# A two-layer hybrid decoder on one core: the second mixer's steps handed out in smaller portions, half of a set of weight sums moved to GpSimd in a later stage, and the value product's weight splits reordered

## The chip, the cores and the metric

The kernel runs on one core of one Trainium2 chip. The metric is device time in microseconds (us) of one execution; lower is better. The engines are named as in the profile: PE is TensorE, PEld its weight loads, DVE is VectorE, ACT is ScalarE, POOL is GpSimd, SP is SyncE, whose queue issues nearly all DMAs here.

## The reference, cut to what matters

The input is 1024 positions of 1024 channels in fp32. Two residual layers follow each other, each a token mixer and a SwiGLU feed-forward, and a last RMSNorm.

```python
for layer in range(2):
    hn = rms_norm(h, norm_mix_g[layer])
    h = h + (mixer_ab if layer == 0 else mixer_cd)(hn, ...)
    hn = rms_norm(h, norm_ffn_g[layer])
    h = h + (silu(hn @ w_gate) * (hn @ w_up)) @ w_down
...
def mixer_cd(h, w_in, lower_bound, norm_g, w_out):
    hq, hf, hi, hg, sq, sk, sv = split_cols(h @ w_in, CD_SPLITS)
    o_c = hgrn2_recurrence(silu(hq), k_in, hi, log_f)       # 4 heads
    o_c = rms_norm(o_c, norm_g) * sigmoid(hg)
    # three dilated windows of attention over sq, sk, sv, 4 heads each, joined by a softmax of their sums
    return concatenate([o_c, o_d]) @ w_out
```

## The kernel before

**Products.** Weights and activations are fp32. Each is split into a rounded part and a rest (`split`, lines 103 and 104: one ACT cast, one DVE subtraction), and each product is three matmuls of 128x128 weights on 512 columns (`mm3`, lines 136 to 138: hi with hi, hi with lo, lo with hi; the third of each group is the first to read the weights' rest).

**Seven products for eight.** The gate and up projections (`Up`), and most of the second mixer's input projection (`Local`), are computed by a scheme of the Strassen kind: two weight blocks and two halves of positions are combined by sums so that seven products of a quarter each do for eight. Both run as a loop of "pairs". One pair is 84 matmuls. Inside it the order of PE, DVE, ACT, POOL and SP is written out by hand (`manual_schedule`): every engine, and SP's queue of DMAs, takes its instructions in the order in which the function `pair` names them. `Local` has pairs 3 to 15 in its loop (15 is the last); the products of one pair run in the order `p1`, `p2`, `end21` and `end12` of the pair before, `p6`, `p5`, `p7`. `p6` and `p5` need the weights `s2`, `s1`, which come from `sums(an, bn)` (POOL, lines 338 and 339, issued late in the pair before), then `part_b` (an ACT cast and a DVE subtraction). `sums` needs the raw weight block `bn`, whose load SP issues in the middle of a pair (`raw`, line 311). `sums_late` (POOL, lines 343 and 344) makes two more. In pairs 12 to 15 four results go through `rope`: two ACT copies, a POOL multiplication (line 873), then a DVE addition that is only issued at the next `flush`.

**The value weights' sums.** The product that makes the recurrence's values (`rows`) uses the same scheme on four weight blocks. Their sums `vsum`, two halves of 1024 columns, are made earlier, in layer 0's `Up`: `block_load` brings 256 columns of four blocks into the single buffer `sd`, `block_sums` runs four DVE operations and stores the result. The same two functions also make `Up`'s own 22 blocks of `w_down` sums. In the pairs of `more` (4 to 15 in layer 0) they run a second time in the pair.

**rows.** After the last pair, `rows` runs the value product, `v_ask` loading a raw weight, `v_unit` splitting it into one of four ring buffers. It ends with the splits of `t1`, needed later by the mixer.

**The second mixer** (`mixer_cd`). Two generators are interleaved with plain projections: `hgrn` (the recurrence, 80 steps) and `local` (attention). `tick(cost)` gives each a credit (3.5 and 2 or 2.5 per 24 matmuls, capped at 3) and runs as many steps as the credit pays. `swa_v` and `hgrn_gates` call it between groups of matmuls. Here no order is written by hand: the tile scheduler orders the instructions by its own estimate, those named earlier first.

Of the kernel before, what the change touches and what calls it, by code (L numbers as in the profile page):

```python
# [56 lines left out]
def hybrid_trunk_kernel(ctx: ExitStack, tc: tile.TileContext, x_t, w_all, w_down, w_ba, vecs, c_f, c_i, c_rope, out):  # L57
# [233 lines left out]
    class Up:  # L291
# [168 lines left out]
        def block_load(self):  # L460
            n = self.blocks - ND // SB
            if n < (0 if self.layer else 2 * DM // SB):
                a = self.right.tile([P, 4, SB], F32, tag="sd", name="sd", bufs=1)
                if n < 0:
                    c = slice(self.blocks * SB, (self.blocks + 1) * SB)
                    dma(a, w_down[self.layer].rearrange("x y p n -> p (x y) n")[:, :, c])
                    d = self.sums_d.rearrange("s p n -> p s n")[:, :, c]
                else:
                    i, c = n // (DM // SB), slice(n % (DM // SB) * SB, (n % (DM // SB) + 1) * SB)
                    for j, at in enumerate(VSETS):  # L470
                        dma(a[:, j], w_all[W_AT["cd", at + i]][:, c])
                    d = vsum[:, i].rearrange("s p n -> p s n")[:, :, c]
                self.block = d, a
                self.blocks += 1
# [30 lines left out]
        def pair(self, f, b11, b21, b22, t1, t2, t3, t4):  # L505

            n = f + 1
            more = (5, 7, 9, 11) if self.layer else range(4, 16)
            self.p1(f, b11)
# [254 lines left out]
    class Local(Up):  # L764

        def __init__(self, left):
            self.left, self.n = left, 0
            self.qk = {k: dr.tile([2 if k[0] is not None else 4, P, T_LEN], F32, name=f"qk{i}")
                       for i, k in enumerate(PAIRS)}
            self.b12 = dr.tile([P, KH, HT], F32, name="b12")  # L770
            self.units = {f: {} for f in range(len(PAIRS) + 1)}
            self.x, self.y, self.z, self.u2, self.g1, self.c22 = {}, {}, {}, {}, {}, {}
            self.snaps = self.right = None
            self.adds, self.stores, self.decays = [], [], {}

        def source(self, kind, f):
# [173 lines left out]
        def run(self, tr, row, b11, b21, hx, close, left, right):  # L950

            self.early(hx)
            E = mybir.EngineType
            engines = {E.PE, E.DVE, E.Activation, E.Pool}
            with tc.manual_schedule(engines=engines):
                b22, t3, t4 = self.turn(tr, row, b11, b21, hx, close, left, right)
            t1, t2 = self.t12
            with tc.manual_schedule(engines=engines | {E.SP}):
                last = len(PAIRS) - 1
                for f in range(3, last + 1):  # L960
                    self.pair(f, f == last, b11, b21, b22, t1, t2, t3, t4)
                self.copy22(last)
                self.add22(last)
                self.end21(last, t4)
                self.rope22(last)
                self.v_unit()
                self.end12(last, b22)
                self.rows(last, b11, b21, b22, t1, t2, t3, t4)
            return [t1, b22], self.vu[14:]

        def v_ask(self):
            i = len(self.vraw)
            if i < 14:
                name, k = ("cd", 8), i % 2
                blk = (8, 10, 0, 2, 3, 1, 46)[i // 2]
                src = w_all[W_AT["cd", blk + k]] if blk >= 8 else vsum[blk, k]
            elif i < 16:
                src = w_all[W_AT["cd", 48 + i - 14]]
            raw = self.left.tile([P, DM], F32, tag="spare", name="raw", bufs=1) if i % 3 == 0 else \
                ring.tile([P, DM], F32, tag="raw", name="raw", bufs=2)  # L980
            dma(raw, src)
            self.vraw.append(raw)

# [6 lines left out]
        def rows(self, last, b11, b21, b22, t1, t2, t3, t4):  # L990
# [9 lines left out]
            def zt():  # L1000
                return self.right.tile([P, HT], F32, tag="z", name="z", bufs=3)

            x = [psu(), psu()]
            for j in range(2):
                prod(x[j], 0, b11, j, first=True)
            self.rope21(last)
            self.add12(last)
            self.v_ask()
            self.v_unit()
            self.rope12(last)  # L1010
            self.v_ask()
            x += [psu(), psg()]
            for j in range(2, 4):
                prod(x[j], 0, b11, j, first=True)
            self.v_unit()
            while self.adds or self.stores:
                self.flush()
            self.v_ask()

            g, y = [], []  # L1020
            for j in range(4):
                y.append(psm())
                prod(y[j], 2, b21, j, first=True, end=True)
                g.append(zt())
                S.copy(g[j], x[j])
                if j > 1:
                    self.v_unit()
                    self.v_ask()
                V.tensor_tensor(g[j], g[j], y[j], op=ADD)
                store(3, 0, j, g[j])  # L1030

            u2 = []
            for n in range(2):
                for j in range(4):
                    prod(x[j], 4, t2, j, range(2 * n, 2 * n + 2))
                if n == 0:
                    self.v_unit()
                    self.v_ask()
            for j in range(4):
                u2.append(self.scratch("u2"))  # L1040
                S.copy(u2[j], x[j])
            self.v_unit()
            self.v_ask()
            for n in range(2):
                for j in range(4):
                    prod(x[j], 6, t3, j, range(2 * n, 2 * n + 2))
                self.v_unit()
                self.v_ask()

            def late(j):  # L1050
                c = self.right.tile([P, HT], F32, tag="c", name="c", bufs=2)
                S.copy(c, x[j])
                return c

            for a in (0, 2):
                z = []
                for j in (a, a + 1):
                    z.append(psm())
                    prod(z[-1], 8, t1, j, first=True)
                    c = late(j)  # L1060
                    V.tensor_tensor(c, c, z[-1], op=ADD)
                    store(1, 1, j, c)
                if a == 0:
                    self.v_unit()
                    self.v_unit()
                    self.v_ask()
                    self.v_ask()
                else:
                    self.v_unit()
                    self.v_unit()  # L1070
                    back = [ring.tile([P, DM], F32, tag="raw", name="raw", bufs=2) for _ in range(2)]
                    for i, raw in enumerate(back):
                        dma(raw.rearrange("p (k t) -> p k t", k=2), self.b12[:, 2 * i:2 * i + 2, :])
                for i, j in enumerate((a, a + 1)):
# [3 lines left out]
            for j in range(4):  # L1078
                prod(x[j], 12, t4, j, end=True)
                if j < 2:  # L1080
                    c = slice(2 * j, 2 * j + 2)
                    split(t1[0][:, c, :], t1[1][:, c, :], back[j].rearrange("p (k t) -> p k t", k=2))
                if j == 1:
                    self.v_ask()
                    self.v_ask()
                c = zt()
                S.copy(c, x[j])
                store(1, 0, j, c)
                if j > 1:
                    self.v_unit()  # L1090

        def pair(self, f, last, b11, b21, b22, t1, t2, t3, t4):
# [8 lines left out]
            else:  # L1101
                self.vraw, self.vu = [], []
                self.v_ask()
                self.v_ask()
            self.add22(f - 1)
            self.decay(f - 1, 4)
            self.part_b(f, self.s)
            self.sums_late(self.a, self.b, self.s)
            self.p2(f, b21, psm())
            g = self.snap(f)  # L1110
# [9 lines left out]
            self.p6(f, t2)  # L1120
            self.rope21(f - 1)
            self.part_d(f, self.a)
            self.decay(f - 1, 6)
            if not last:
                bn = self.raw("u", n, n % 3 == 2)
            self.add12(f - 1)
            if not last:
# [4 lines left out]
            if last:  # L1132
                self.v_unit()
                self.v_ask()
            self.rope12(f - 1)
# [954 lines left out]
    def mixer_cd(hn, hp, qkd, wv):  # L2090
# [5 lines left out]
        with ExitStack() as es:  # L2096
# [16 lines left out]
            def halves_of(w, half, tick):  # L2113
                o = proj(w, hn[half], range(KH), last=False)
                tick(0.5)
                return proj(w, hn[half], range(KH, KT), o, first=False)

# [147 lines left out]
            def hgrn_gates(tick):  # L2265
                ws = [wload(("cd", 12 + 2 * i), ("cd", 13 + 2 * i)) for i in range(2)]
                for h in range(4):
                    for half in range(NH):
# [7 lines left out]
                        gate_store[0] = dma(catd[half][h], xg).ins  # L2276
                        tick(0.5)


            def swa_v(p, tick, w=()):  # L2280
# [14 lines left out]
                for tts in ((0, 1, 2), (3,), (4,), (5, 6, 7)):  # L2295
                    os_ = [psu() for _ in tts]
                    for ks in ((range(0, 2), range(2, 4), range(4, 6), range(6, 8)) if len(tts) > 1 else (range(KT),)):
                        for tt, o in zip(tts, os_):
                            part(o, tt, ks)
                        tick(0.75 if len(tts) > 1 else 1)  # L2300
                    for tt, o in zip(tts, os_):
# [540 lines left out]
```

## Time and profile before

| | us |
|---|---|
| three runs | 2521.59, 2521.28, 2519.64 |
| median of the runs | 2521.28 |
| the profiled execution | 2526.62 |
| its span, first to last instruction | 2524.5 |

The span is what the rows below are taken from; the profiled execution has 2.1 us more around it and is 5.3 us above the median of the runs. PE is busy for 2491.4 us of the span.

### The profile page before, as it was taken

How to read it: one execution, taken by the hardware profiler on the slowest of the kernel's cores; microseconds unless marked ns; L12 is line 12 of the kernel's file. 1: busy time of each engine (PE TensorE's matmuls, PEld its weight loads, DVE VectorE, ACT ScalarE, POOL GpSimd, SP SyncE). 2: the span in 40 equal slices, each digit the busy share in tenths (PEclk: the TensorE clock that was granted, in tenths of full speed). 3: DMA queues.
4: the chain of work that ended last, by engine and by line, in shares of the span. 5: the costliest groups of instructions: out<-in, count | busy, mean ns of one | idle time of the engine just before them, and what ended most of it. 6: DMA issues, size and time to landing. Idle time of an engine off the chain costs nothing. (4 is left out here: it accounts for less than half of the span.)

```text
span 2524.5 us, 37197 instructions
## 1 busy us (share of the span) xinstructions
PE 2491.4 (99%) x13715; PEld 2062.4 (82%) x13715; DVE 1695.4 (67%) x2823; ACT 1100.7 (44%) x1932; POOL 637.4 (25%) x591
## 2 busy tenths in 40 slices
PE   9999999999999999999999999999999999999998
PEld 7888888888887888888888877788788888888887
DVE  8987776676566565567798636678668565656554
ACT  5432134343333344344676535567535333334442
POOL 1311112333333400031566300010132333330001
PEclk9999999999999999999999999999999999999999
DMA  4535457335667688544344456776732555668853
GB/s 156 163 121 169 133 174 264 104 117 193 207 226 238 215 302 292 183 139 137 129 142 153 138 174 219 185 211 195 255 134 93 183 184 192 204 213 287 277 177 125
DMA packets 296526, 467.20 MB, mean 185 GB/s; under 512 B 50168, under 2 KB 151064, under 8 KB 296088
## 3 DMA queue, kind: packets, MB, share of 16 engines
q1 hardware_dynamic: 296056, 464.31, 56.6%
q8 instruction: 107, 1.75, 0.3%
q10 hardware_dynamic: 288, 0.52, 0.1%
q14 instruction: 75, 0.61, 0.1%
HBM read 314.18 MB, written 150.55 MB: 184 GB/s over the span
## 5 line engine op out<-in xcount | busy, mean ns | idle before, releaser
L104 DVE TENSOR_TENSOR w<-raw,w 128x1024 fp32r<-128x1024 f32 (+1 forms) x333 | 400.4, 1205 | 155.0 <-ACT w L103 153.5
L103 ACT CAST w<-raw 128x1024 fp32r<-128x1024 f32 (+1 forms) x333 | 315.3, 954 | 280.6 <-PE psu L138 126.2
L136 PE MATMUL psu<-hnh,w 128*128 128x512 f32 x772 | 308.3, 399 | 0.0
L138 PE MATMUL psu<-hnh,w 128*128 128x512 f32 x772 | 301.3, 390 | 0.0
L137 PE MATMUL psu<-hnl,w 128*128 128x512 f32 x772 | 301.3, 390 | 0.0
L199 POOL TENSOR_TENSOR acc<-acc,sq 128x512 f32<-128x512 f32 x52 | 78.8, 1516 | 440.3 <-ACT sq L195 440.2
L338 POOL TENSOR_TENSOR ws<-raw 128x512 f32<-128x512 f32 x54 | 71.2, 1319 | 452.3 <-DMA raw<-in_dram 271.5
L136 PEld LDWEIGHTS psu<-hnh,w 128*128 128x128 f32 x772 | 145.1, 188 | 31.0 <-ACT sq L195 0.8
L138 PEld LDWEIGHTS psu<-hnh,w 128*128 128x128 f32 x772 | 145.0, 188 | 30.9
L137 PEld LDWEIGHTS psu<-hnl,w 128*128 128x128 f32 x772 | 145.2, 188 | 28.2
L104 DVE TENSOR_TENSOR hidq<-hr,hidq 128x1024 fp32r<-128x1024 f32 x72 | 82.3, 1145 | 78.7 <-ACT hidq L103 78.4
L104 DVE TENSOR_TENSOR w<-ws,w 128x1024 fp32r<-128x1024 f32 x51 | 71.8, 1408 | 89.8 <-ACT w L103 89.8
L103 ACT CAST hidq<-hr 128x1024 fp32r<-128x1024 f32 x72 | 70.2, 980 | 103.2 <-DMA hr<-ts 62.4
L429 POOL TENSOR_TENSOR hid<-hid,c 128x512 f32<-128x512 f32 x44 | 64.7, 1470 | 168.6 <-ACT hid L428 168.5
L136 PE MATMUL psm<-hidq,w 128*128 128x512 f32 (+1 forms) x275 | 106.1, 386 | 0.0
L137 PE MATMUL psm<-hidq,w 128*128 128x512 f32 (+1 forms) x275 | 105.8, 385 | 0.0
L138 PE MATMUL psm<-hidq,w 128*128 128x512 f32 (+1 forms) x275 | 105.8, 385 | 0.0
L136 PE MATMUL psu<-t3h,w 128*128 128x512 f32 x240 | 93.8, 391 | 4.4 <-ACT u L401 4.3
L381 ACT ACTIVATE gt<-gt 128x512 f32<-128x512 f32 x44 | 27.8, 632 | 155.2 <-DVE gt L378 155.2
L136 PE MATMUL psu<-t4h,w 128*128 128x512 f32 x240 | 93.5, 390 | 0.8 <-ACT c L890 0.8
L137 PE MATMUL psu<-t3l,w 128*128 128x512 f32 x240 | 93.4, 389 | 0.0
L137 PE MATMUL psu<-t4l,w 128*128 128x512 f32 x240 | 93.4, 389 | 0.0
(614 smaller groups left out, 6700.6 us busy)
## 6 DMA issues: line engine op xcount, KB each, us to landing
raw<-in_dram SPq DMA_DIRECT2D x223, 512.0 KB, 4.4
sd<-in_dram SPq DMA_DIRECT2D x44, 512.0 KB, 4.0
hid<-hid SPq DMA_DIRECT2D x88, 256.0 KB, 3.3
sd<-sd SPq DMA_DIRECT2D x44, 512.0 KB, 3.0
hr<-ts SPq DMA_DIRECT2D x40, 512.0 KB, 4.7
raw<-sd SPq DMA_DIRECT2D x40, 512.0 KB, 4.7
qk<-z SPq DMA_DIRECT2D x52, 256.0 KB, 3.1
hd<-h SPq DMA_DIRECT2D x48, 256.0 KB, 2.9
```

The costliest lines, as they stand in the source:

```text
L103: S.copy(hi, src)
L104: eng.tensor_tensor(lo, src, hi.bitcast(F32), op=SUB)
L136: T.matmul(o, lh, rh, start=first and i == 0, stop=False, **kw)
L137: T.matmul(o, lh, rl, start=False, stop=False, **kw)
L138: T.matmul(o, ll, rh, start=False, stop=last and i == n - 1, **kw)
L199: (eng or G).tensor_tensor(a, a, q, op=ADD)
L338: G.tensor_tensor(s[:, HT:], b[:, :HT], b[:, HT:], op=ADD)
L381: S.activation(self.g1[f], self.g1[f], AF.Silu)
L429: G.tensor_tensor(h, h, self.c22.pop(f), op=MULT)
```

## The change

Three edits. (1) `tick` is called behind every six matmuls with a quarter of the cost, in `swa_v` and in `hgrn_gates`; the sum of the costs is the same. (2) Layer 0's `Up` makes only the first half of `vsum`; its second calls in a pair end at pair 11. The other half is loaded in `Local`, in pairs 13 and 14, as eight blocks of 128 columns, four DMAs each, and is summed by POOL: each `v_sums` runs four POOL operations and a store per block loaded since the last one. (3) The loads and splits of the value product are asked for earlier and more evenly, its raw weights have four buffers and not three, and the product's first half moves ahead of the last pair's `end21` and `end12`.

```diff
         def block_load(self):
             n = self.blocks - ND // SB
-            if n < (0 if self.layer else 2 * DM // SB):
+            if n < (0 if self.layer else DM // SB):
...
-            more = (5, 7, 9, 11) if self.layer else range(4, 16)
+            more = (5, 7, 9, 11) if self.layer else range(4, 12)
...
+        def v_load(self, f):
+            for i in range(2 if 13 <= f < 15 else 0):
+                n = len(self.vblocks)
+                c = slice(n * P, n * P + P)
+                a = self.scratch("vs").rearrange("p (s n) -> p s n", s=4)
+                for j, at in enumerate(VSETS):
+                    dma(a[:, j], w_all[W_AT["cd", at + 1]][:, c])
+                self.vblocks.append((a, vsum[:, 1].rearrange("s p n -> p s n")[:, :, c]))
+
+        def v_sums(self):
+            t = G.tensor_tensor
+            for a, d in self.vblocks[self.vdone:]:
+                t(a[:, 3], a[:, 2], a[:, 3], op=ADD)
+                t(a[:, 2], a[:, 0], a[:, 2], op=SUB)
+                t(a[:, 0], a[:, 3], a[:, 0], op=SUB)
+                t(a[:, 1], a[:, 1], a[:, 0], op=SUB)
+                dma(d, a)
+            self.vdone = len(self.vblocks)
...
+        def v_raw(self):
+            i = len(self.vraw) % 4
+            raw = ring.tile([P, DM], F32, tag="raw", name="raw", bufs=2) if i in (1, 2) else \
+                self.left.tile([P, DM], F32, tag=("spare", None, None, "s")[i], name="raw", bufs=1)
...
+            def nxt():
+                self.v_unit()
+                self.v_ask()
...
             x = [psu(), psu()]
+            self.copy22(last)
+            self.add22(last)
             for j in range(2):
                 prod(x[j], 0, b11, j, first=True)
+            self.end21(last, t4)
+            self.rope22(last)
+            self.end12(last, b22)
             self.rope21(last)
             self.add12(last)
-            self.v_ask()
-            self.v_unit()
+            nxt()
...
             self.part_b(f, self.s)
             self.sums_late(self.a, self.b, self.s)
+            self.v_sums()
+            self.v_load(f)
             self.p2(f, b21, psm())
...
             self.rope21(f - 1)
+            self.v_sums()
+            self.v_load(f)
             self.part_d(f, self.a)
             self.decay(f - 1, 6)
             if not last:
                 bn = self.raw("u", n, n % 3 == 2)
+            else:
+                self.v_ask()
+                self.v_ask()
...
             if last:
-                self.v_unit()
-                self.v_ask()
+                for _ in range(2):
+                    self.v_unit()
+                    self.v_ask()
...
             def halves_of(w, half, tick):
-                o = proj(w, hn[half], range(KH), last=False)
-                tick(0.5)
-                return proj(w, hn[half], range(KH, KT), o, first=False)
+                o = psu()
+                for k in range(0, KT, 2):
+                    if k:
+                        tick(0.25)
+                    proj(w, hn[half], range(k, k + 2), o, first=k == 0, last=k == KT - 2)
+                return o
...
-                        tick(0.5)
+                        tick(0.25)
...
-                    for ks in ((range(0, 2), range(2, 4), range(4, 6), range(6, 8)) if len(tts) > 1 else (range(KT),)):
+                    for ks in (range(0, 2), range(2, 4), range(4, 6), range(6, 8)):
                         for tt, o in zip(tts, os_):
                             part(o, tt, ks)
-                        tick(0.75 if len(tts) > 1 else 1)
+                            tick(0.25)
```

## Rows read from the trace of the kernel before

**Rows 1.** The page, span and busy times of PE

```profile
span 2524.5 us, 37197 instructions
...
PE 2491.4 (99%) x13715; PEld 2062.4 (82%) x13715; DVE 1695.4 (67%) x2823; ACT 1100.7 (44%) x1932; POOL 637.4 (25%) x591
```

**Rows 2.** Stretches: us, busy by engine (xcount), granted clock, DMA share, GB/s

```profile
740.00:830.00 90.00, 85.61 (x374) 69.61 (x373) 57.95 (x79) 30.98 (x44) 34.97 (x24) 1.00 0.70 229
...
1190.00:1364.00 174.00, 174.00 (x770) 144.06 (x769) 145.04 (x167) 127.19 (x180) 99.65 (x66) 1.00 0.44 142
...
1422.00:1515.00 93.00, 89.63 (x483) 73.02 (x482) 39.85 (x53) 34.04 (x46) 6.96 (x8) 1.00 0.52 174
1515.00:1800.00 285.00, 269.47 (x3142) 227.43 (x3141) 214.09 (x753) 179.00 (x517) 26.19 (x47) 0.98 0.70 202
1542.70:1549.50 6.80, 6.03 (x17) 4.98 (x18) 1.94 (x6) 3.49 (x11) 0.00 (x0) 0.50 0.63 192
1631.40:1638.30 6.90, 5.12 (x92) 4.38 (x93) 6.48 (x18) 5.30 (x15) 1.69 (x4) 0.51 0.50 162
```

**Rows 3.** In order of time, layer 0's `Up`: start, duration, instruction, [idle before, releaser]

```profile
770.59 1.76 SPq L471 DMA_DIRECT2D sd<-in_dram  x4
...
776.37 0.43 DVE L479 TENSOR_TENSOR sd<-sd 128x256 f32<-128x256 f32 x1 [5.29 <-DMA raw<-in_dram]
...
785.63 0.50 PE L136 MATMUL psu<-t3h,w 128*128 128x512 f32 x1 [1.95 <-ACT u L401]
```

**Rows 4.** PE's waits from 1360 to 1515: us in total, times, longest

```profile
PE psm L137 <- DVE w L104: 1.8, 1, 1.8
PE psu L136 <- ACT c L890: 0.8, 1, 0.8
```

**Rows 5.** In order of time, `Local`, pairs 13 and 14

```profile
1380.50 1.29 POOL L873 TENSOR_TENSOR sw<-sw,rope 128x512 f32<-128x512 f32 x1 [2.76 <-ACT sw L872]
...
1382.41 0.33 SPq L311 DMA_DIRECT2D raw<-in_dram  x1
...
1386.65 1.29 POOL L338 TENSOR_TENSOR ws<-raw 128x512 f32<-128x512 f32 x1 [1.05 <-DMA raw<-in_dram]
...
1390.43 1.22 DVE L104 TENSOR_TENSOR w<-ws,w 128x1024 fp32r<-128x1024 f32 x1 [4.55 <-ACT w L103]
1390.53 2.28 POOL L344 TENSOR_TENSOR raw<-raw,ws 128x512 f32<-128x512 f32 x1
...
1394.76 0.39 PE L136 MATMUL psu<-t2h,w 128*128 128x512 f32 x1
```

**Rows 6.** Groups on POOL by shape: busy us, mean ns of one, idle before

```profile
L338 POOL TENSOR_TENSOR ws<-raw 128x512 f32<-128x512 f32 x54 | 71.2, 1319 | 452.3 <-DMA raw<-in_dram 271.5 <-DVE hid L456 77.5 <-DVE gt L378 45.2
...
L1917 POOL COPY yt<-yd 32x128 f32<-32x128 f32 x32 | 10.6, 343 | 35.0 <-DMA yd<-scr_y 26.8 <-DVE y L1867 7.5
...
L2005 POOL TENSOR_TENSOR ss<-ss,s_nq 128x4 f32<-128x4 f32 x8 | 2.1, 267 | 57.3 <-ACT oq L1999 57.3
```

**Rows 7.** SP's queue, its waits from 1360 to 1425

```profile
SPq L311 <- DVE w L104: 10.3, 2, 5.3
```

**Rows 8.** PE's waits in the second mixer, 1510 to 1800

```profile
PE psg L2259 <- DVE e L2254: 2.2, 3, 1.2
PE psg L2225 <- ACT e L2220: 1.9, 2, 1.1
```

**Rows 9.** PE in order of time: two waits, and a visit to small matmuls

```profile
1513.61 0.50 PE L138 MATMUL psu<-w,hnl 128*128 128x512 f32 x1
1513.95 0.39 PE L136 MATMUL psu<-w,hnh 128*128 128x512 f32 x1
1514.27 0.76 PE L2158 MATMUL psg<-m 128*32 128x32 f32 x64
...
1543.47 0.69 PE L2418 MATMUL psm<-cf,sc 128*128 128x128 f32 x2 [2.71 <-ACT sc L2375]
...
1631.69 0.66 PE L2158 MATMUL psg<-m 128*32 128x32 f32 x32 [2.86 <-DVE m L2150]
```

More of the change, by code (lines that the diff above doesn't have):

```diff
@@ L468, in block_load @@
                 else:
-                    i, c = n // (DM // SB), slice(n % (DM // SB) * SB, (n % (DM // SB) + 1) * SB)
+                    c = slice(n * SB, (n + 1) * SB)
                     for j, at in enumerate(VSETS):
-                        dma(a[:, j], w_all[W_AT["cd", at + i]][:, c])
-                    d = vsum[:, i].rearrange("s p n -> p s n")[:, :, c]
+                        dma(a[:, j], w_all[W_AT["cd", at]][:, c])
+                    d = vsum[:, 0].rearrange("s p n -> p s n")[:, :, c]
                 self.block = d, a
@@ L774, in __init__ @@
             self.adds, self.stores, self.decays = [], [], {}
+            self.vblocks, self.vdone = [], 0
         def source(self, kind, f):
@@ L961, in run @@
                     self.pair(f, f == last, b11, b21, b22, t1, t2, t3, t4)
[L962 to L965, printed above, removed]
-                self.v_unit()
-                self.end12(last, b22)
                 self.rows(last, b11, b21, b22, t1, t2, t3, t4)
             return [t1, b22], self.vu[14:]
-        def v_ask(self):
[L972 to L982, printed above, removed]
+        def v_load(self, f):
[19 more added lines that the diff above has]
+                self.left.tile([P, DM], F32, tag=("spare", None, None, "s")[i], name="raw", bufs=1)
+            self.vraw.append(raw)
+            return raw
+        def v_ask(self):
+            i, k = len(self.vraw), len(self.vraw) % 2
+            blk = (8, 10, 0, 2, 3, 1, 46, 48)[i // 2]
+            dma(self.v_raw(), w_all[W_AT["cd", blk + k]] if blk >= 8 else vsum[blk, k])
         def v_unit(self):
@@ L1001, in zt, with back @@
                 return self.right.tile([P, HT], F32, tag="z", name="z", bufs=3)
+            def nxt():
+                self.v_unit()
+                self.v_ask()
+            def back(n):
+                dma(self.v_raw().rearrange("p (k t) -> p k t", k=2), self.b12[:, 2 * n:2 * n + 2, :])
             x = [psu(), psu()]
+            self.copy22(last)
+            self.add22(last)
             for j in range(2):
                 prod(x[j], 0, b11, j, first=True)
+            self.end21(last, t4)
+            self.rope22(last)
+            self.end12(last, b22)
             self.rope21(last)
             self.add12(last)
-            self.v_ask()
-            self.v_unit()
+            nxt()
             self.rope12(last)
-            self.v_ask()
             x += [psu(), psg()]
@@ L1014, in rows @@
                 prod(x[j], 0, b11, j, first=True)
-            self.v_unit()
+            nxt()
             while self.adds or self.stores:
                 self.flush()
-            self.v_ask()
             g, y = [], []
@@ L1025, in rows @@
                 S.copy(g[j], x[j])
-                if j > 1:
-                    self.v_unit()
-                    self.v_ask()
                 V.tensor_tensor(g[j], g[j], y[j], op=ADD)
                 store(3, 0, j, g[j])
+                if j > 1:
+                    nxt()
             u2 = []
@@ L1036, in rows @@
                 if n == 0:
-                    self.v_unit()
-                    self.v_ask()
+                    nxt()
             for j in range(4):
@@ L1041, in rows @@
                 S.copy(u2[j], x[j])
-            self.v_unit()
-            self.v_ask()
+            nxt()
             for n in range(2):
@@ L1046, in rows @@
                     prod(x[j], 6, t3, j, range(2 * n, 2 * n + 2))
[L1047 to L1053, printed above, removed]
+                nxt()
+                if n == 1:
+                    nxt()
             for a in (0, 2):
@@ L1059, in rows @@
                     prod(z[-1], 8, t1, j, first=True)
-                    c = late(j)
+                    c = self.right.tile([P, HT], F32, tag="c", name="c", bufs=2)
+                    S.copy(c, x[j])
+                    if j == 0:
+                        nxt()
                     V.tensor_tensor(c, c, z[-1], op=ADD)
                     store(1, 1, j, c)
-                if a == 0:
+                if a:
+                    nxt()
                     self.v_unit()
[L1065 to L1073, printed above, removed]
+                    back(0)
                 for i, j in enumerate((a, a + 1)):
@@ L1080, in rows @@
                 if j < 2:
[L1081 to L1085, printed above, removed]
+                    self.v_unit()
+                    if j == 0:
+                        back(1)
                 c = zt()
@@ L1088, in rows @@
                 store(1, 0, j, c)
-                if j > 1:
-                    self.v_unit()
+            for n in range(2):
+                c = slice(2 * n, 2 * n + 2)
+                split(t1[0][:, c, :], t1[1][:, c, :], self.vraw[16 + n].rearrange("p (k t) -> p k t", k=2))
         def pair(self, f, last, b11, b21, b22, t1, t2, t3, t4):
@@ L1103, in pair @@
                 self.v_ask()
-                self.v_ask()
             self.add22(f - 1)
@@ L1132, in pair @@
             if last:
-                self.v_unit()
-                self.v_ask()
+                for _ in range(2):
+                    self.v_unit()
+                    self.v_ask()
             self.rope12(f - 1)
```

## The prediction, made before the changed kernel ran

> **What bounds the kernel.** The page first: PE is busy for 2491.4 us of a span of 2524.5 [rows 1]. The change takes no matmul away, so all it can win is PE's idle time, 33.1 us, and time at a lower clock; all it can lose is new waits. The stretches come next [rows 2]. In `Local` from 1190 to 1364 PE is never idle: 770 matmuls in 174 us, 0.226 us each, so a pair of 84 takes 19.0 us. Idle time lies in three places that the change touches: layer 0's `Up` from 740 to 830 (90.0 less 85.6: 4.4 us), `rows` from 1422 to 1515 (3.4 us) and the second mixer from 1515 to 1800 (15.5 us). In the mixer the granted clock also stood at 0.5, which is 1.2 GHz, for two spells of 6.8 and 6.9 us; PE's busy part of them, 6.0 and 5.1 us, would take half as long at 2.4 GHz: 5.6 us more. The reader is to see that everything to be won is about 29 us, and that `Local` has nothing to win.
>
> **Layer 0's Up.** The idle time there begins at the buffer `sd`: SP spends 1.76 us on issuing the four loads of one block of `vsum`, DVE stands for 5.29 us until the loads of that time have landed (the profile names a raw load), and PE's `p7` then waits 1.95 us for an ACT copy that is queued behind DVE's late work [rows 3]. The edit takes four such blocks away and gives each pair from 12 on one block where it had two, so that a load has half a pair or more before DVE asks. I take the whole 4.4 us as won: **-4.4** (bounds 0, if another load is late in its place, and -4.4). DVE's 16 operations and 16 loads that go are hidden under PE and win nothing themselves.
>
> **rows.** Two waits go [rows 4]. The 0.8 us for ACT's copy of the last pair's sum goes because 24 matmuls are put between it and `end21`. The 1.8 us for a split is that of the two weights of `b22`, which were both split after the first products of `t1`; in the new order the later of them is split 12 matmuls ahead. **-2.6** (bounds 0 and -2.6). Behind it the splits of `t1` come last, but their first use is after two sets of projections in the mixer, over 20 us later.
>
> **The second mixer.** The sum of the credits is the same, but bursts go: two attention steps in a row, or `ms1` and `od1` of the recurrence in a row, now have 12 matmuls between them, and every other two steps of one generator at least six. The two longest waits are of just this kind: 2.71 us for exponentials just issued and 2.86 us for `m` [rows 9]; two more groups, 2.2 and 1.9 us, wait for a result of the step just before [rows 8]. They won't all go: DVE is busy for 214 of 285 us [rows 2], and the tile scheduler had already moved matmuls between steps where it foresaw a wait (the visit at 1514.27 lies in the middle of a group). I take two thirds of 15.5 us: **-10** (bounds: nothing, and all 15.5). Each spell at half clock began beside one of the two long waits; without them I count the clock as full: **-5.6** (bounds 0 and -5.6). Against it stand more changes between big and small matmuls. Counted through the code, 36 groups of matmuls were followed by a step with work for PE, and now some 70 are. Around a visit one big matmul takes 0.34 and one 0.32 us to the next start [rows 9] where 0.226 is normal: 0.21 us together, of which most visits, to wider small matmuls, should pay about half. 34 times 0.1: **+3.4** (bounds 0 and 7).
>
> **Local, the sums on POOL.** No row shows a 128x128 sum on POOL. A two-operand POOL instruction takes 0.27 us with 4 columns and 1.29 to 1.32 us with 512 [rows 5, 6]; on the line between them 128 columns take 0.51. Eight, for the two blocks of one `v_sums`, take 4.1 us. Bounds: 0.34 each, as a copy of 128 columns [rows 6], and 0.64, a quarter more, since `sums_late` beside busy DVE took 2.28 instead of 1.29 [rows 5]. I take 0.51, the line through the same kind of instruction. The GPSIMD Engine Reference of the Trainium skill (section 3.1) speaks against such sums on this engine and gives 4497 ns for 2048 columns; scaled down with no fixed cost that is an estimate of 0.28 us each, and by it the `Local` term below would be about 9 us instead of 16.8; the trace's 1.29 us for 512 columns, where that scale gives 1.12, speaks for a fixed cost on top.
>
> These 32 operations are on POOL, which has room for one `v_sums` a pair, but what counts is SP. SP's queue takes its DMAs in order and already stands for 10.3 us in two waits of raw loads [rows 7]. In pairs 13 and 14 the second `v_sums` puts two stores, which wait for POOL, and eight loads in front of the load of `bn`, and `bn` is what the next pair's `sums` needs.
> - Pair 13: POOL's third rope multiplication ends at 1381.8; eight sums, 4.1, to 1385.9; one store 0.4 and eight loads at 0.44 [rows 3], 3.5, to 1389.8. There `bn` is issued, before at 1382.4. From issue to POOL's first sum took 4.2 us (1382.41 to 1386.65), and from there to the end of the split 5.0 (1391.65) [rows 5]: 1399.0. `p6` begins at 1394.76 and its third matmul needs the split's rest 0.45 later: a wait of 3.8 us. Behind the waiting ACT cast stand the copy of `p1` and the ropes, so nothing else feeds PE meanwhile.
> - Pair 14 has four blocks, and POOL and SP form a loop: `sums` and `sums_late` 6.2 (1386.65 to 1392.81), four-operation sums of two blocks 4.1, two ropes 2.6, ACT's copies 0.6, the third rope 1.3, two more blocks 4.1, store and loads 3.9, landing 4.2: 27.0 us, against a pair of 19.0. `sums` starts at 1394.0 + 27.0 = 1421.0, its split is done at 1426.0, and `p6` of pair 15, due at 1394.76 + 19.04 + 0.45 = 1414.25, is 11.8 us late, the 3.8 included.
> - Pair 15: POOL again has `sums_late`, two blocks and two ropes before DVE may go on (1421.0 + 6.2 + 4.1 + 2.6 = 1433.9); two DVE operations of 0.7, the last part of the pair's own weights 0.7, an addition 0.7, then the first value weight's rest 1.2: 1437.9. PE is through with pair 15 at 1433.7 and waits 3.8 more; the second value weight, whose load stands behind POOL's stores in SP's queue, costs 1.2 more. Together 5.0.
>
> **+16.8** (bounds 9, with 0.34 us a sum and SP's issues at 0.33, and 21, with 0.64). Without the cover of the 3.5 us that the split had to spare before `p6`, all of it would be 3.5 more. Dearer or cheaper, the price is in the two loops, not in the 16 us of work on POOL.
>
> **The sum.** -4.4 - 2.6 - 10 - 5.6 + 3.4 + 16.8 = -2.4 us on a profiled 2526.6; on the median of the runs, 2521.3, that is 2518.9 us. 0.2%, about what a measurement of this kernel can tell from no change, is 5.0 us.
>
> **The rivals.**
> - A, *the queue absorbs it*: POOL's sums are as cheap as their lower bound and the raw load's delay in pair 14 is mostly the slack of 3.5 us, so `Local` loses 5 or less. For it: before the change POOL is busy for only 99.65 of 174 us there [rows 2]. Against: 27.0 us for the loop leaves 8 us to be explained away. -2.4 - 11.8 = -14.2: 2507 us.
> - B, *the mixer keeps its waits* (slower). The scheduler reorders by its own estimate, so the same wrong estimates give the same waits at other places, and the visits cost their 3.4. For it: all of the 15.5 us but the two long waits lies in waits of 1.2 us and less [rows 8], most of them for DVE, which is no freer. It decides as soon as the mixer wins less than 5 us in all: -4.4 - 2.6 + 16.8 + 3.4 - 3 = +10.2: 2531 us.
> - C, *the clock falls again*: each spell at half clock stands beside a PE wait of 2.7 us or more [rows 2, 9], and pairs 14 and 15 get waits of 3.8, 8 and 3.8. Spells of 6.8 us there would cost 3.4 each where no later wait takes them up; the loops take up two, one is left: 2522 us. TensorE: Matmul & The Clock Gate (the Trainium skill, "HAM oscillation") has it that the clock is throttled anew at every such wait and each is paid for; by that rule, three spells with nothing to take them up, the time would be about 10 us over the sum. For the two spells that this trace has, at granted 0.50 and 0.51, it agrees.
> - D, *nothing moves*: PE's waits in `Up` and the mixer go and as much comes back in `Local`, or neither: 2521 us.
>
> **Chances.** The forecast 0.45, between 2510 and 2526, half of it faster by over 0.2% and half not; A 0.2, faster; B 0.2, slower; C 0.1, half within 0.2% and half slower; D 0.05. Faster: 0.22 + 0.2 = 0.42. Same: 0.23 + 0.05 + 0.05 = 0.33. Slower: 0.2 + 0.05 = 0.25. The predicted time is the forecast's, 2519. The range reaches to A and B: 2505 to 2531; the forecast's own is 2510 to 2526.
>
> **What would show it.** Right: no wait of PE for `u` between 740 and 830; in pairs 14 and 15 PE waits of about 4 and 8 us before `p6`, for a DVE rest whose POOL sum waited for a raw load, with that load issued 7 us later in its pair than before; a wait for the first value weight; PE idle for some 5 us in the mixer and its clock full. Wrong: PE busy without a break through pairs 13 to 15 (the `Local` term fails, A), or an idle time of over 12 us in the mixer (B). A POOL sum of 128 columns far from 0.51 us would mis-size the `Local` term, by 32 times the difference and no more than that along the loops.

## The result and the profile after

The changed kernel is slower: 2526.43 us in the median of 16 runs (2524.45 to 2528.30) against 2521.44 (2514.74 to 2523.98), a ratio of 1.0023 with a 95% interval of [1.0015, 1.0031], or 5.0 us. The forecast was 2.4 us faster.

The two profiled executions say the opposite, spans of 2522.9 and 2524.5 us. The profiled execution of before, 2526.62 us, lies above all of its 16 timed runs, so differences between the two traces are read here by stage, and the experiments time each edit by itself. The stretches of the changed kernel, with the columns of [rows 2]:

```profile
740.00:830.00 90.00, 90.00 (x398) 74.51 (x397) 53.78 (x70) 30.04 (x43) 31.25 (x25) 1.00 0.59 201
1360.00:1440.00 80.00, 64.68 (x256) 50.58 (x254) 38.50 (x48) 31.10 (x47) 52.69 (x56) 0.89 0.44 140
1392.60:1399.40 6.80, 4.68 (x11) 3.63 (x12) 4.40 (x5) 4.90 (x7) 6.57 (x7) 0.50 0.00 0
1419.90:1430.20 10.30, 5.59 (x13) 4.36 (x14) 4.40 (x5) 4.97 (x8) 9.42 (x10) 0.50 0.20 80
...
1528.00:1815.00 287.00, 282.30 (x3317) 238.13 (x3316) 224.91 (x771) 186.12 (x528) 28.54 (x50) 1.00 0.77 227
```

Layer 0's `Up` has lost all its idle time, and the mixer (last row) has 4.7 us of it where [rows 2] has 15.5, at the full clock. `Local`, which never waited before, now has PE idle for 15.3 of 80 us (the last 2.1 of them at the start of `rows`) and two spells at the lower clock. PE's waits over the whole kernel, longest in total first:

```profile
PE psu L136 <- ACT gt L374: 12.2, 2, 6.7
PE psu L136 <- DVE z L884: 2.6, 1, 2.6
PE psg L2245 <- ACT e L2240: 2.3, 4, 0.8
PE psu L137 <- DVE w L104: 1.7, 2, 1.6
...
PE psu L130 <- ACT w L103: 0.8, 1, 0.8
```

The two waits of 12.2 us together are those before `p6` of pairs 14 and 15. They are put down to ACT's copy `gt`, which stands on ACT behind the cast that waits for the sums. The loop behind it, in order of time over several engines:

```profile
1376.04 0.91 POOL L978 TENSOR_TENSOR vs<-vs 128x128 f32<-128x128 f32 x1
...
1377.57 1.32 POOL L980 TENSOR_TENSOR vs<-vs 128x128 f32<-128x128 f32 x1
1378.97 0.46 POOL L981 TENSOR_TENSOR vs<-vs 128x128 f32<-128x128 f32 x1
...
1381.00 0.46 POOL L981 TENSOR_TENSOR vs<-vs 128x128 f32<-128x128 f32 x1
...
1379.45 2.40 SPq L982 DMA_DIRECT2D vsum<-vs  x2
1381.95 3.81 SPq L972 DMA_DIRECT2D vs<-in_dram  x8
1385.85 0.38 SPq L311 DMA_DIRECT2D raw<-in_dram  x1
...
1390.50 1.26 POOL L338 TENSOR_TENSOR ws<-raw 128x512 f32<-128x512 f32 x1 [7.79 <-DMA raw<-in_dram]
...
1394.72 0.80 PE L136 MATMUL psu<-t2h,w 128*128 128x512 f32 x1 [5.52 <-ACT gt L374]
...
1420.39 1.26 POOL L338 TENSOR_TENSOR ws<-raw 128x512 f32<-128x512 f32 x1 [7.71 <-DMA raw<-in_dram]
...
1424.61 0.80 PE L136 MATMUL psu<-t2h,w 128*128 128x512 f32 x1 [6.65 <-ACT gt L374]
...
1436.21 0.49 PE L136 MATMUL psu<-w,hnh 128*128 128x512 f32 x1 [0.56 <-ACT w L103]
1438.27 0.50 PE L137 MATMUL psu<-w,hnh 128*128 128x512 f32 x1 [1.57 <-DVE w L104]
```

The reader is to see the order: eight sums on POOL, two stores that wait for them, eight loads, only then the raw load. POOL itself idles 7.79 us for the load that its own sums held up. From `sums` to `sums` the loop takes 29.9 us (1390.50 to 1420.39), where a pair of matmuls takes 19.0. SP's own waits from 1375 to 1440 are nearly all of this one kind:

```profile
SPq L982 <- POOL vs L981: 40.0, 8, 11.7
```

By stage, from the starts of PE's matmuls (the first of `Up`'s pair 4, of `Local`'s pairs 4, 14 and 15, of the recurrence, and the first at line 130 behind it, in layer 1's `Up`), in us:

| stage | before | changed | difference |
|---|---|---|---|
| layer 0's `Up` from its pair 4, up to pair 4 of `Local` | 636.9 | 631.3 | -5.6 |
| pair 14 | 19.04 | 28.16 | +9.1 |
| pair 15 and rows | 110.3 | 122.5 | +12.2 |
| mixer and what follows | 303.0 | 285.2 | -17.8 |

### The profile page after: what moved, and what is told of

The parts are those of the page before. It is cut to its first block, busy times and chain, and to the rows that moved or that the text cites. A ratio compares the mean times of both kernels' runs of the same rounds, so it can differ in the third digit from the quotient of the medians.

```text
span 2522.9 us, 37281 instructions
## 1 busy us (share of the span) xinstructions
PE 2490.0 (99%) x13715; PEld 2060.9 (82%) x13715; DVE 1688.9 (67%) x2807; ACT 1102.4 (44%) x1932; POOL 645.6 (26%) x623
## 5 line engine op out<-in xcount | busy, mean ns | idle before, releaser
L136 PE MATMUL psu<-t2h,w 128*128 128x512 f32 x228 | 90.9, 399 | 12.2 <-ACT gt L374 12.2
L344 POOL TENSOR_TENSOR raw<-raw,ws 128x512 f32<-128x512 f32 x51 | 78.8, 1544 | 57.3 <-DVE w L104 54.9
```

Of the source, the lines that this page charges most:

```text
L136: T.matmul(o, lh, rh, start=first and i == 0, stop=False, **kw)
L344: G.tensor_tensor(a[:, HT:], a[:, HT:], s[:, :HT], op=SUB)
```

## The experiments

Each differs from the kernel before or from the changed one as its diff says.

**The kernel before again.** No edit.

> The kernel before, unchanged. Theory 1, its profiled execution was an unlucky one in the second mixer (two long waits, two spells at half clock): here the stretch from the mixer's first recurrence matmul to the end of the mixer is 297 us or less instead of 303, and the span lies near 2519. Theory 2, the profile is typical: the stretch is again 302 to 304 us and both spells are there.

2522.59 us; the mixer's stretch took 300.0 us. Its row, to be read beside that of [rows 2] from 1515 on (the first line is this run, 1505 to 1800; PE idle 13.3 us):

```profile
1505.00:1800.00 295.00, 281.69 (x3287) 236.62 (x3286) 222.90 (x768) 184.94 (x525) 30.51 (x50) 0.98 0.70 208
```

Neither theory's number was met: 300 lies between. But the four other traces of kernels with the old mixer agree on the direction, 297.3 to 299.2 us in the three below (edits 2, 3, and 3 with swapped banks). The profiled execution of before is the longest of five here, by 3 to 6 us, and this is most of why the traces and the runs differ in sign.

**Edit 1 alone.** The three hunks of `halves_of`, `hgrn_gates` and `swa_v`.

```diff
-                        tick(0.75 if len(tts) > 1 else 1)
+                            tick(0.25)
```

> Edit 1 alone: steps behind every six matmuls. Theory 1 (typical executions of before lose less in the mixer than the profiled one): 9 to 13 us faster than before in the runs, the mixer's stretch 285 to 288 us, its clock full. Theory 2 (the traces' difference is what the runs have): 17 us faster. Rival B of the prediction: no gain, or a loss of 3.

0.9949 [0.9937, 0.9962], 2507.74 against 2520.30: 12.6 us faster. The mixer's stretch is 285.6 us, and its row shows the full clock:

```profile
1512.00:1800.00 288.00, 282.78 (x3321) 238.79 (x3320) 226.24 (x771) 186.37 (x527) 28.66 (x51) 1.00 0.76 226
```

Rival B of the prediction, that the waits only move, is out.

**Edit 2 alone.** `block_load` and `more` as in the change, `v_load` and `v_sums` in `pair`; nothing else.

> Edit 2 alone: half of the value weights' sums on POOL in pairs 13 to 15. Theory 1, the loop of POOL and SP is the whole loss: 14 to 17 us slower than before (Up gives 4 to 6 back, pairs 14 and 15 lose 9 each and the first value weights are 1 to 4 late). Rival, the loss is taken up again in the rows behind it: 5 to 9 slower.

1.0076 [1.0063, 1.0090], 2539.46 against 2520.30: 19.2 us slower, beyond both expectations. `Up` takes 631.3 us (4.1 less than in the run of before above), so what `Local` and the rows lose is 23 us: pair 14 takes 28.2 again, and pair 15 with the rows 123.8 against 109.4.

**Edit 3 alone.** The hunks of `run`, `v_ask`, `rows` and the last pair.

> Edit 3 alone: the value product's splits reordered, its first half ahead of end21 and end12. As predicted: 2.6 us faster, both waits gone. Rival, from the changed kernel's trace, where the product's third PSUM bank waits 2.6 us for the rope of the last pair: no difference, the two old waits gone and this one new.

0.9999 [0.9990, 1.0008]: no difference. Both waits of [rows 4] are gone, and from 1400 to 1512 PE has one wait, a new one:

```profile
PE psu L136 <- DVE z L883: 2.6, 1, 2.6
```

Edits 1, 2 and 3 by themselves give -12.6, +19.2 and -0.6 us, +6.0 together; the change as a whole measured +5.0.

**The raw load first.** The changed kernel; in `pair`, the second `v_sums` and `v_load` stand behind the load of `bn`.

```diff
             self.rope21(f - 1)
-            self.v_sums()
-            self.v_load(f)
             self.part_d(f, self.a)
...
                 bn = self.raw("u", n, n % 3 == 2)
...
+            self.v_sums()
+            self.v_load(f)
             self.add12(f - 1)
```

> The changed kernel with the second sums and block loads of pairs 13 and 14 put behind the raw load of the next pair, so that this load waits for no POOL store; POOL's work and order stay. Theory 1, the loop through SP is most of the loss in pairs 13 to 15: 11 to 15 us faster than the changed kernel (2511 to 2515 us); pair 14 takes 19 to 22 us and not 28, and what is left is POOL's own 22.8 us of work in pair 14 and the late first value weights. Rival, POOL's own load is the loss: 2 to 6 us faster.

0.9968 [0.9956, 0.9981], 2512.35 us: 14.1 us below the changed kernel's median, with POOL's work unchanged. Pair 14 takes 20.4 us. The raw load goes out 9.1 us earlier, ahead of the stores, and POOL goes on without a break:

```profile
1376.71 0.33 SPq L311 DMA_DIRECT2D raw<-in_dram  x1
1379.48 2.42 SPq L982 DMA_DIRECT2D vsum<-vs  x2
1381.99 3.81 SPq L972 DMA_DIRECT2D vs<-in_dram  x8
...
1381.46 1.29 POOL L874 TENSOR_TENSOR sw<-sw,rope 128x512 f32<-128x512 f32 x1
1382.71 1.28 POOL L338 TENSOR_TENSOR ws<-raw 128x512 f32<-128x512 f32 x1
```

So the loop through SP, and not POOL's load as such, is most of the loss. What is left is 1.4 us in pair 14 and 9.7 in pair 15 and the rows (118.8 against 109.0 with edit 3 alone). It begins at POOL, which has more than a pair's worth of work in pair 14: from `sums` to `sums` 22.2 us pass, 1382.71 to 1404.95, with one pause of 0.8. In the rows PE waits 2.4 and 1.5 us for the first value weight, whose split stands behind ropes that POOL makes after its sums, and the clock falls to 0.50 for 6.8 and 3.4 us there; half of PE's busy time in these spells, an estimate of what they cost, is 4.6 us.

**Without POOL's sums.** The changed kernel; each block is loaded and stored unsummed, so half of the value weights' sums are left out.

```diff
             for a, d in self.vblocks[self.vdone:]:
-                t(a[:, 3], a[:, 2], a[:, 3], op=ADD)
-                t(a[:, 2], a[:, 0], a[:, 2], op=SUB)
-                t(a[:, 0], a[:, 3], a[:, 0], op=SUB)
-                t(a[:, 1], a[:, 1], a[:, 0], op=SUB)
                 dma(d, a)
```

> The changed kernel without the four sums per block on POOL (the blocks are loaded and stored unsummed, so half of the sums of the value weights are left out); loads, stores and their place in SP's queue stay. Theory 1, a loop that needs both: with nothing of POOL to wait for, the stores and loads go out before the raw load's buffer is free, and pair 14 takes 19.0 us, the span is 2503 to 2507 us. Rival, SP's ten issues in front of the raw load cost by themselves: pair 14 takes 20 to 22 us.

One run: 2504.69 us, span 2502.6, pair 14 19.0 us, pair 15 and the rows 111.0. All of SP's issues are still there and still ahead of the raw load; they are over at 1376.68, and the load goes out 0.1 us later, less than 0.4 us behind its place in the kernel with the raw load first:

```profile
1371.43 1.05 SPq L978 DMA_DIRECT2D vsum<-vs  x2
1372.53 4.15 SPq L972 DMA_DIRECT2D vs<-in_dram  x8
1376.79 0.36 SPq L311 DMA_DIRECT2D raw<-in_dram  x1
```

The larger part of the loss needs both: a store that waits for POOL, and a load that POOL needs behind it in one queue. With POOL's sums and the load ahead of the store, 7.7 us of it stay (2512.35 against this one run).

**Edit 3, banks swapped.** The third and fourth PSUM bank of the value product in the other order.

```diff
-            x += [psu(), psg()]
+            x += [psg(), psu()]
```

> Edit 3 alone, and the third and fourth PSUM banks of the value product taken in the other order (first the one that is free), so that the bank held by the last pair's rope is asked for 12 matmuls later. If the wait of 2.6 us for that bank is what ate edit 3's gain: 2 to 3 us faster than the kernel before, and no wait for DVE's z in the rows. Rival, the wait only moves on to the next bank: no difference, as with edit 3 alone.

0.9982 [0.9973, 0.9990], 2516.01 against 2519.81: 3.8 us faster by the medians. The wait for `z` is gone; pair 15 and rows take 106.3 us (109.0 with edit 3 as it is).

**A version that beats both.** Edits 1 and 3 with the banks swapped; layer 0 makes six of the eight blocks, POOL only the last 512 columns, one set of two small blocks in each of pairs 13 and 14, behind the raw load.

```diff
-            if n < (0 if self.layer else DM // SB):
+            if n < (0 if self.layer else 6):
...
-            more = (5, 7, 9, 11) if self.layer else range(4, 12)
+            more = (5, 7, 9, 11) if self.layer else range(4, 14)
...
             self.sums_late(self.a, self.b, self.s)
-            self.v_sums()
             self.v_load(f)
...
-            self.v_sums()
-            self.v_load(f)
             self.part_d(f, self.a)
...
                 bn = self.raw("u", n, n % 3 == 2)
...
+            self.v_sums()
```

> Edit 1; edit 3 with the banks in the other order; and a quarter, not half, of the sums moved to POOL: layer 0 makes six of eight blocks with second calls to pair 13, POOL one set of two small blocks in each of pairs 13 and 14, behind the raw load. If the terms add up, -12.7 for the mixer, -4 for layer 0 and -2.6 for the rows on 2520: 2499 to 2503 us, PE without a wait in pairs 13 to 15. Rival, POOL's 5.4 us in a pair already delay the next pair's sums beyond their slack: 2504 to 2510.

0.9925 [0.9911, 0.9938], 2501.88 against 2519.81: 17.9 us faster than before. `Up` has 1.0 us of idle time left and `Local` none:

```profile
740.00:830.00 90.00, 88.98 (x393) 73.33 (x392) 54.53 (x76) 31.72 (x45) 32.57 (x26) 1.00 0.65 220
1360.00:1440.00 80.00, 80.00 (x353) 65.83 (x352) 51.26 (x64) 40.95 (x61) 49.58 (x44) 1.00 0.49 165
```

POOL is busy for 49.58 of those 80 us, 3 less than in the changed kernel, and delays nothing: the terms add up once the order is right.

**Where edit 1's gain lies.** First the value projections alone, then the gates alone.

> Edit 1 in the value projections alone (swa_v), the gates as before. The waits of the old mixer lie two thirds and more in this part, and the spells at half clock too: 8 to 11 us faster than before, if the gain is the bursts' waits where they stood. Rival, the finer portions only help where attention and recurrence meet the gates: 0 to 4 faster.

> Edit 1 in the gates alone (steps behind 6 instead of 12 matmuls). If gains go by the waits of each part: 2 to 4 us faster than before. Rival: no difference, since 12 matmuls between steps are enough.

0.9970 [0.9960, 0.9980] and 0.9988 [0.9979, 0.9997]: 7.6 and 3.0 us by the ratios. Their sum, 10.6, and the 12.9 of edit 1's ratio agree within the intervals. In the second run of the kernel before, 8.8 us of PE's idle time in the mixer lie in the value part and 4.5 behind it, so the gains go about as the waits do.

**Every twelve matmuls.** The value projections call `tick(0.5)` behind every second group of six.

```diff
-                        tick(0.75 if len(tts) > 1 else 1)
+                            sixes[0] += 1
+                            if sixes[0] % 2 == 0:
+                                tick(0.5)
```

> The value projections hand out steps behind every twelve matmuls (half of the cost each) and not 18 or 24; the gates as before. The attention then gets one step at a time, the recurrence still one or two. If two attention steps in a row are the costly burst: the same 8 to 11 us as with six matmuls. If the recurrence's bursts count as much: 3 to 6.

0.9966 [0.9954, 0.9979], 8.6 us, as much as with six in this part (its interval holds the other's ratio). The attention then runs one step at a time and the recurrence still up to two; that parting attention steps is what pays fits, but the two versions were not told apart.

**One more empty step.** On the version that beats both: a second `yield` behind the recurrence's transposes, rate 3.85 for 3.5.

> The best version (edit 1, edit 3 with the banks in the other order, a quarter of the sums on POOL) with one more empty step between the recurrence's transposes and the matmul that reads ACT's copy of them, and a rate of 3.85 instead of 3.5 for the 88 steps. If the wait of 3.3 us that is left there is a matter of distance: 2 to 3 us faster than the best version (2499 to 2500). Rival, the other steps come closer and wait instead: no difference or 2 slower.

0.9925 [0.9913, 0.9938], 2500.09 us. The wait for `e` at the next matmul fell from 3.3 to 0.5 us, others of up to 1.0 us came in its place, and no difference to the version before can be told.

## Why the prediction was wrong

**Layer 0's Up (-4.4) was right.** Idle time is gone from 740 to 830, and the stage takes 631.3 or 631.4 us in the four traces with the whole of edit 2 and 633.8 to 636.9 in the eight with the old `Up`.

**The mixer (-12.2 in all) came out in the runs**, 12.6 us by medians and 12.9 by the ratio, where the trace of before alone would have said 17.8. But its terms did not, and that the sum fits is in part luck. The profiled execution had more idle time and more time in spells than the others: in the four other traces of the old mixer PE idles for 11.9 to 13.8 us, in those with edit 1 in both parts for 4.7 to 5.6, so 6 to 9 us were won and not 10, and half of PE's busy time in the spells is 2.6 to 4.4 us and not 5.6. Against it the changes between big and small matmuls, put at +3.4, cost nothing that can be seen. PE goes from a 512-column matmul to a smaller one 53 times in the mixer of before and 68 times in the changed one, where the code's count gave 36 and some 70, and its time outside idle time and spells is 281.2 us before (282.3 to 282.7 in the four others) and 280.5 after. What was too much on one side made up for what was not there on the other. The clock's spells went with the waits, as argued: no trace with edit 1 in both parts has one in the mixer, and each of the five with the old mixer has one or two.

**Rows (-2.6) failed.** Both old waits went, but edit 3 makes its own, of 2.6 us: the last pair's `end21` moves behind 24 matmuls, so its rope moves too, and the third PSUM bank of the product is the one that this rope frees. The prediction followed who fills the weights and not who frees the banks. The bank swap shows it.

**Local (+16.8) had the right mechanism, and its size was off**: 23 us (edit 2 alone, 19.2 plus the 4.1 that `Up` gives back), above even the bound of 21. The step that failed is the price of a sum on POOL, "the line through the same kind of instruction", 0.51 us for each of the eight. The trace has, by line:

```profile
L980 POOL TENSOR_TENSOR vs<-vs 128x128 f32<-128x128 f32 x8 | 7.1, 890 | 0.6
L978 POOL TENSOR_TENSOR vs<-vs 128x128 f32<-128x128 f32 x8 | 4.6, 572 | 0.0
L979 POOL TENSOR_TENSOR vs<-vs 128x128 f32<-128x128 f32 x8 | 3.7, 460 | 0.6
```

For a sum that nothing disturbs the price was right: 0.46 us long, and four in a row start 0.51 apart (1378.97 to 1381.00). But in each set one or two sums begin while DVE splits a weight, and take 0.91 and 1.32 (the last section has the rows). So the eight of pair 13 take 5.4 us from the first's start to the end of the last, not 4.1, or 0.68 for each sum. [rows 5] had shown this in `sums_late`, 2.28 beside a split instead of 1.29: one whole microsecond on one instruction, which the forecast left out for the new sums and the bound spread over them as a quarter each. The estimate by the GPSIMD Engine Reference of the Trainium skill (section 3.1), 0.28, was off further.

Store and loads took 4.4 us and not 3.9 (1381.46 to 1385.85), the landing 4.65 and not 4.2. The loop of pair 14 has two sets of sums, 4.9 and 5.4 us, and took 29.9 us where 27.0 was worked out; 2.2 of the 2.9 are the sums. Pair 14 became 9.1 us longer, and `p6` of pair 15 began 16.5 us late (46.45 us behind the start of pair 14, in the trace of before 29.92), where 11.8 was predicted. In the two waits PE stood for ACT's `gt` and not, as the prediction's sign had it, for DVE's rest of the split; both stand behind the same cast. The waits for the value weights are 2.3 us and not 5.0, since PE came later to them: with 0.50 granted for part of the way, it took 11.0 us for `p6`, `p5` and `p7` of pair 15 and not 8.2. These 2.9 and the 2.3 make 5.2, so this part of the term fits.

**Rival C** did occur: the clock fell in both new waits, of 5.5 and 6.65 us, to 0.50, which is 1.2 GHz. At the full clock the 4.68 and 5.59 us that PE was busy in the spells would have been half, 5.1 us less. No run takes the spells away by themselves, but the rows fit the prediction's view that the loops take them up. From 1390.50 to the end of the second set at 1411.44 POOL's only pause is 0.77 us, for ACT copies that waited for DVE and not for PE; and what PE lost in pair 15 it would have waited for the value weight instead. **Rival A** is out (pair 14 at 28.2 us).

The errors add: about 6.5 in `Local` and 2.6 in the rows turn -2.4 into +6.7; the runs have +5.0.

## What to carry to other kernels

Before moving work to an idle engine, write down the queue that its stores go through and what stands behind them: a store that waits for the engine, ahead of a load which the same engine needs next, makes a loop, and every price in it is paid in each turn; putting the load first won 14 us with no work moved. Price the moved work beside what the other engines do at that time, and not only by itself. Where products are moved, follow who frees the PSUM banks as well as who fills the weights. And take a second profile of the kernel before when the terms are a few tenths of a per cent: one unlucky execution can turn the sign.

## What the runs showed of the hardware that was not expected

A POOL sum that begins while DVE splits a weight is not some tenths dearer but up to nearly three times. Two like sums in one set, the third operation of each block, and DVE at the time of the first; then a sum beside other DVE work:

```profile
1397.61 1.32 POOL L980 TENSOR_TENSOR vs<-vs 128x128 f32<-128x128 f32 x1
...
1400.50 0.46 POOL L980 TENSOR_TENSOR vs<-vs 128x128 f32<-128x128 f32 x1
...
1397.15 1.46 DVE L104 TENSOR_TENSOR w<-raw,w 128x1024 fp32r<-128x1024 f32 x1
...
1379.93 0.46 POOL L979 TENSOR_TENSOR vs<-vs 128x128 f32<-128x128 f32 x1
...
1379.69 0.68 DVE L897 TENSOR_TENSOR psm<-c,psg 128x512 f32<-128x512 f32 x1
```

The one that starts while DVE splits a weight takes 1.32 us, and the one with DVE idle (its next instruction begins at 1402.78) 0.46. DVE being busy is not enough: a split reads both operands from SBUF, and beside an addition that reads one from PSUM (L897) the sum takes 0.46 too. And the sum is not slowed by a share, it is held: all six long sums of this trace end 0.31 to 0.32 us behind the end of the split (here 1398.93 and 1398.61), whether 0.6 or 1.0 us of it were left. The GPSIMD Engine Reference of the Trainium skill (section 2, Architecture) says that the one read and one write port of each of its cores are shared with DVE. The trace agrees with a shared resource that one of the two holds; no run here separates the ports from another cause.

SP takes 3.81 us to issue eight loads of 64 KB, 0.48 each, no less than the 0.44 of the ones of [rows 3], which are twice as large: smaller pieces made the queue longer and saved it nothing.
